# Loading the direct terms of the state space layer from the weights' queue, between the weights of the feed-forward network ahead of it

## The chip, the cores and the metric

The kernel runs on one core of a Trainium2 chip. The metric is device time in microseconds (us) of one launch. The engines of the core are TensorE (PE; its weight loads are listed apart as PEld), VectorE (DVE), ScalarE (ACT), GpSimd (POOL) and SyncE (SP); each executes its own row of instructions strictly in the order in which they stand. Transfers are issued from SP, ACT and POOL.

## What is computed

A stack of layers on a sequence of 256 tokens with 1024 features, in float32: stick-breaking attention, spatial gating, a state space layer (S5), attention again, each followed by a gated feed-forward network (FFN) with a short convolution; then a second block. What matters here is the second of these FFNs, called ffn1, and the S5 layer after it:

```
def conv_gated_ffn(xn, w_up, conv_w, conv_b, w_down):
    h = causal_depthwise_conv(xn @ w_up, conv_w, conv_b)
    a, g = jnp.split(h, 2, axis=-1)
    return (jax.nn.silu(g) * a) @ w_down
...
def s5_layer(...):
...
    _, _, xr, xi = lax.associative_scan(_complex_affine_combine, (a_re, a_im, bu_re, bu_im), axis=1)
    y = (jnp.einsum('ghp,blgp->blgh', c_re.astype(jnp.float32), xr)
         - jnp.einsum('ghp,blgp->blgh', c_im.astype(jnp.float32), xi))
```

The kernel computes the S5 scan in chunks of 8 tokens. Inside a chunk the answer of a group of 16 channels to its own inputs is one 128 x 128 matrix per group; these 64 matrices are the direct terms, `dT`. They depend on parameters alone.

## The kernel before

Activations lie transposed, features on the partitions. A matrix product is done in three passes for accuracy: the weights are split into a high and a low part (`wh`, `wl`), the activations too (`yh`, `yl`, or `hh`, `hl` for the hidden layer), and a block of 128 x 128 weights costs three matmuls of 256 columns, in the order `wh` with the high activations, `wh` with the low ones, `wl` with the high ones (`mm3`, L516 to L518).

**The stream of weights.** Eight blocks make a unit. For each unit there is one DMA of 512 KB on SP's queue (`_dma`, L352) into one of five staging tiles `st`, one ACT instruction that makes `wh` (L374), one DVE instruction that makes `wl` (L375), and then 24 matmuls. SP may load into `st` again when the `wl` of the unit that lay there is made. There are five `wh` and five `wl` tiles.

**ffn1** has 66 units, counted here from 0. `ffn_walk` goes through them as `ffn_order` says: 22 parts of the hidden layer, two units each (j = 0 to 21), and between them, from j = 4 on, the down products of parts that are done, two units after each pair of parts. So units 36 and 37 are part 13, units 38 and 39 a down product, 40 and 41 part 14. When PE has done part j, its activation follows as a chain over DVE and ACT (`act` in `ffn`): `pr` (DVE, L722), two `cv` on ACT (L725), four `cv` on DVE (L727), `sg` (ACT, L730), `hm` (DVE, L732), `hh` (ACT, L542), `hl` (DVE, L543).

**Work beside ffn1.** Tables and matrices that the S5 layer needs of its parameters are computed during the layers ahead of it, by a chain of generators `s.pre`, one of which is stepped on where `pre_step` is called (each step has a price, and a call pays for some). The last three are `s5_pre2` (products `O` and `A` on DVE, stored to `dB`), `s5_tables` (`s5mag`, `s5sin`, `s5cos`: DVE and ACT) and `s5_direct`: sixteen DMAs of 256 KB that read the matrix `dK` in device memory with a shift and write `dT`, issued by POOL (L1204). S5 uses `dT` in `y_mm` (L1302).

**What sets the order.** The code gives the instructions in program order with priorities; a scheduler of the tile layer then arranges each engine's row ahead of the run, by estimates of its own of when things become ready. `tc.keep_in_program_order` keeps an instruction from being moved on its engine. Once the program is built the rows are fixed.

Of the kernel before, what the change touches and what calls it, by code (L numbers as in the profile page):

```python
# [35 lines left out]
SBA, SBB, SBC = 4, 3, 1  # L36
EVG = 2
NSTEP = (2, 3)
DTC = 0.3
FEND = ((0, (18, 20)), (1, (18, 20)), (2, (18, 20)), (0, (20, 22)), (1, (20, 22)), (2, (20, 22)), (3, (18, 22)))  # L40
LATE = ((0, 1, 2, 3), (4, 5))
CY = (5, 2, 3, 2)
# [241 lines left out]
class Build:  # L284
    def __init__(s, ctx, tc, I, out, off, phases):
        s.tc, s.nc, s.I, s.out, s.ctx = tc, tc.nc, I, out, ctx
        nc = s.nc
        pool = lambda name, bufs, **k: ctx.enter_context(tc.tile_pool(name=name, bufs=bufs, **k))
        s.cp = pool("cp", 1)
        s.whp = pool("whp", WB)  # L290
        s.stp = pool("stp", NST)
        s.cq = pool("cq", 1)
        s.wlp = pool("wlp", WB)
        s.wk = pool("wk", 2)
        s.mm = pool("mm", MMB, space=PSUM)
        s.zp = pool("zp", 2, space=PSUM)
        s.pz = pool("pz", 1, space=PSUM)
        s.dp = pool("dp", 1, space=DRAM)
        s.bg = []
        s.pre = None  # L300
        s.credit = 0.0
        s.ahead = set()
        s.sin = None
        s.lowp = 0
        s.pin = 0
        s.want = 0
        s.phases = phases

        s.plan = []
        s.pos = -1  # L310
        s.cur = None
        s.ndma = 0
        s.nsp = 0
        s.tiles = {}

        w = I["consts"].shape[1]
        s.cp.tile([128, 48], F32, tag="gap", name="gap")
        s.cst = s.cp.tile([128, w], F32, tag="cst", name="cst")
        s.c = {k: s.cst[:, o:o + n] for k, (o, n) in off.items()}
        s.gs = s.cp.tile([128, 13 * 8], F32, tag="gs", name="gs")  # L320
        s.conv = s.cp.tile([128, 4, 4, 44], F32, tag="conv", name="conv")
        s.ssq = s.cp.tile([128, 2, T], F32, tag="ssq", name="ssq")
        s.rrow = s.cp.tile([128, T], F32, tag="rrow", name="rrow")
        s.idb = s.cp.tile([128, 128], BF, tag="idb", name="idb")
        s.msb = s.cp.tile([128, 128], BF, tag="msb", name="msb")
        s.msm = s.cp.tile([128, 128], BF, tag="msm", name="msm")
        s.x = s.cp.tile([128, KC, T], F32, tag="x", name="x")
        s.yh = s.cp.tile([128, KC, T], F32R, tag="yh", name="yh")
        s.yl = s.cp.tile([128, KC, T], F32R, tag="yl", name="yl")
        s.mcm = s.cp.tile([128, 2, 16], BF, tag="mcm", name="mcm")  # L330
        s.rcol = s.cq.tile([128, 2], F32, tag="rcol", name="rcol")
        s.g12 = s.cq.tile([128, 8], F32, tag="g12", name="g12")
        s.rcol2 = s.cq.tile([128, 2, 2], F32, tag="rcol2", name="rcol2")
        s.ss = s.cq.tile([128, 3, 2], F32, tag="ss", name="ss")
        s.cq.tile([128, 64], F32, tag="gap", name="gap")
# [336 lines left out]
    def ffn_walk(s, fp, act, resid, side):  # L672

        pre = s.norm_steps()
        P = None
        held = []
        H = {}
        acc = []
        nb = 0
        for x in ffn_order():  # L680
            if x[0] == "u":
                _, j, m, c = x
                if P is None:
                    P = s.ps().rearrange("p (m t) -> p m t", m=2)
                s.mm3(P[:, m], s.blk(), s.yh[:, c], s.yl[:, c], m == 0 and c == 0, c == KC - 1)
                nb += 1
                if nb in FSTEP:
                    next(pre)
                    if nb == FSTEP[1]:
                        pre = None  # L690
                if m == 1 and c == KC - 1:
                    held.append((j, P))
                    P = None
                    while held and pre is None:
                        k, Q = held.pop(0)
                        if k % 2 == 0:
                            H[k // 2] = [fp.tile([128, 2, T], F32R, tag=t, name=t, bufs=HB) for t in ("hh", "hl")]
                        act(k, Q, *[h[:, k % 2] for h in H[k // 2]])
                    if j < side[2]:
                        s.pre_step(side[0])  # L700
            else:
                _, n, c = x
                while not acc or n // 4 >= len(acc):
                    acc.append(s.zt())
                h, l = H[c // 2]
                b = acc[n // 4][:, n // 2 % 2].rearrange("p (m t) -> p m t", m=2)
                s.mm3(b[:, n % 2], s.blk(), h[:, c % 2], l[:, c % 2], n % 2 == 0 and c == 0, c == FT - 1)
                if n % 2 and c == FT - 1:
                    resid(n // 2, b)
                if n % 4 == 3 and c % 2 and c < side[2]:  # L710
                    s.pre_step(side[1])
# [483 lines left out]

    def s5_direct(s):

        while s.cpT is None:
            yield None
        for h in range(2):  # L1200
            s.dT[h] = s.cpT.tile([128, 32, 128], F32, tag="dT%d" % h, name="dT")
            src = s.dK[h * 32:h * 32 + 32, 0:16].rearrange("g h z k -> h g (z k)")
            for j in range(8):
                s.nc.gpsimd.dma_start(s.dT[h][j::8], src[:, :, (8 - j) * 16:(8 - j) * 16 + 128])  # L1204
                yield DTC

    def s5(s, nxt):
        nc = s.nc
# [642 lines left out]
    def run(s):  # L1851
# [15 lines left out]
        if "s5" in ph:  # L1867
            pool1, pool2, pool5 = ExitStack(), ExitStack(), ExitStack()
            tp = s.tc.tile_pool
            cp5 = pool5.enter_context(tp(name="cp5", bufs=1, side="right"))  # L1870
            s.s5cos = cp5.tile([128, 32, 32], F32, tag="s5cos", name="s5cos")
            s.s5sin = cp5.tile([128, 32, 32], F32, tag="s5sin", name="s5sin")
            s.s5mag = cp5.tile([128, 32], F32, tag="s5mag", name="s5mag")
            s.s5th = cp5.tile([128, 32], F32, tag="s5th", name="s5th")
            s.dT = [None, None]
            s.pre2_pool = None
            s.prep_pool = pool1.enter_context(tp(name="pre1", bufs=1))
            s.cpT = None
            s.pre = chain(s.s5_pre(), s.s5_pre2(), s.s5_tables(), s.s5_direct())
            s.pre_step(SIDE[7])  # L1880
        for i, p in enumerate(ph):
            if p == "s5" or "s5" in ph and ph[i + 1:i + 2] == ["s5"]:
                if s.cpT is None:
                    s.cpT = pool5.enter_context(tp(name="cpT", bufs=1, side="right"))
            if "s5" in ph and s.pre2_pool is None:
                s.pre2_pool = pool2.enter_context(tp(name="pre2", bufs=1))
            if p == "s5":
                s.pre_step(1e9)
                pool2.close()
                pool1.close()  # L1890
                if i == 0:
                    s.start_stream()
            nx = gi[ph[i + 1]] if i + 1 < len(ph) else None
            fin = 8 if i + 1 < len(ph) and ph[i + 1] == "mix2" else None
            if "mix2" in ph and i == max(0, ph.index("mix2") - 1):
                rope = ExitStack()
                s.pre = s.rope_tables(rope.enter_context(s.tc.tile_pool(name="rope", bufs=1, side="right")))
                s.credit = 0.0
            if p == "sb0" or p == "sb3":
                s.sb(int(p[2]), nx)  # L1900
            elif p == "sgu":
                s.sgu(nx)
            elif p == "s5":
                s.s5(nx)
                pool5.close()
            elif p == "mix2":
                s.pre_step(1e9)
                ld = s.tc.keep_in_program_order(s.nc.scalar.preload_act_table_set("exp_and_others"))
                with s.tc.issue_after(ld.ins):
                    s.mix2(nx, 8)  # L1910
                rope.close()
            elif p == "ffnx":
                if "ple" in ph:
                    s.ple_load(s.ctx.enter_context(s.tc.tile_pool(name="pl", bufs=1)))
                s.ffnx(nx)
            elif p == "ple":
                s.ple()
            else:
                s.ffn(int(p[3]), nx, fin)
# [28 lines left out]
```

## Time and profile before

| | us |
|---|---|
| median of 2 runs | 1616.78 (1616.11 to 1617.46) |
| profiled execution | 1621.75 |
| its span, first to last instruction | 1619.9 |
| busy PE, PEld, DVE, ACT, POOL | 1574.6, 1512.5, 1303.2, 948.5, 68.9 |

A row of the timeline gives start and length in us, engine, line, operation, what is written and read, and in square brackets how long the engine stood idle before it and what ended that. Rows of the windows give the busy time and the number of instructions of each engine in a stretch, the TensorE clock that was granted there (1.00 is 2.4 GHz, 0.50 is 1.2 GHz, between them a mixture), the share of the DMA engines and GB/s. Matmuls overlap: one row is 0.28 us long, the next starts 0.11 us later. Rows that follow each other on DVE or ACT overlap by about 0.1 us.

### The profile page before, as it was taken

The numbers are of one execution on the slowest core, as the hardware profiler recorded it, in microseconds if no ns is written. First come the engines' busy times: TensorE is split into PE (matmuls) and PEld (weight loads), VectorE is DVE, ScalarE is ACT, GpSimd is POOL, SyncE is SP. The second block draws the span as 40 slices with busy tenths as digits, with TensorE's granted clock in tenths as the row PEclk, the third lists the DMA queues.
The fourth block names the chain that finished last, engine by engine and source line by source line (L and its number), as shares of the span: only waits on it lengthen the run. The fifth ranks groups of instructions, "written<-read, shape, count | busy, mean of one in ns | idle before, by whom it ended". The sixth has DMA issues, their size and how long they took to land.

```text
span 1619.9 us, 33923 instructions
## 1 busy us (share of the span) xinstructions
PE 1574.6 (97%) x13644; PEld 1512.5 (93%) x13644; DVE 1303.2 (80%) x2380; ACT 948.5 (59%) x1481; POOL 68.9 (4%) x118
## 2 busy tenths in 40 slices
PE   7999999989999997999999999999999999999998
PEld 6999999979999996999999999999997899999998
DVE  8999998888999877788788558988886667766666
ACT  6777665645556651666566676655665546554444
POOL 0320100021120000000000000000000000000000
PEclk9999999999999997999999999999999999999999
DMA  7655767697996666756665434666554434666662
GB/s 262 202 172 178 232 210 224 198 298 222 263 252 229 219 194 201 259 173 207 196 195 187 153 129 144 203 201 195 159 174 137 149 112 133 200 192 193 195 195 79
DMA packets 95359, 312.55 MB, mean 193 GB/s; under 512 B 15057, under 2 KB 20689, under 8 KB 95201
## 3 DMA queue, kind: packets, MB, share of 16 engines
q1 hardware_dynamic: 82560, 282.21, 55.1%
q0 software_dynamic: 8480, 27.12, 5.9%
q8 instruction: 107, 1.75, 0.4%
q10 hardware_dynamic: 4160, 1.05, 0.3%
q14 instruction: 52, 0.42, 0.1%
HBM read 297.49 MB, written 12.85 MB: 192 GB/s over the span
## 4 chain that ended last, share of the span: by engine, by line
PE 72%; DVE 10%; issue 9%; DMA 5%; ACT 3%; POOL 0%; DVEq 0%; POOLq 0%; ACTq 0%; SPq 0%
PE mm L516 16%; PE mm L518 15%; PE mm L517 15%; PE z L517 5%; PE z L516 5%; PE z L518 5%; DVE wl L375 3%; DMA A<-s5bT_dram 1%; DMA st<-ffn_dram 1%; PE mm L530 1%; PE mm L531 1%; PE mm L529 1%; ACT wh L374 1%; PE z L818 1%; PE z L805 1%
## 5 line engine op out<-in xcount | busy, mean ns | idle before, releaser
L375 DVE TENSOR_TENSOR wl<-st,wh 128x1024 fp32r<-128x1024 f32 x508 | 618.2, 1220 | 156.1 <-ACT wh L374 155.3
L374 ACT CAST wh<-st 128x1024 fp32r<-128x1024 f32 x508 | 528.7, 1046 | 328.0 <-PE mm L517 207.3
L516 PE MATMUL mm<-yh,wh 128*128 128x256 f32 x2512 | 703.7, 280 | 2.9 <-ACT yh L568 1.9
L517 PE MATMUL mm<-yl,wh 128*128 128x256 f32 x2512 | 698.6, 278 | 1.4 <-DVE yl L569 0.9
L518 PE MATMUL mm<-yh,wl 128*128 128x256 f32 x2512 | 698.4, 278 | 1.0 <-DVE wl L375 1.0
L516 PEld LDWEIGHTS mm<-yh,wh 128*128 128x128 f32 x2512 | 473.5, 189 | 10.7 <-issue 6.4
L517 PEld LDWEIGHTS mm<-yl,wh 128*128 128x128 f32 x2512 | 474.1, 189 | 3.3 <-DVE yl L569 1.7
L518 PEld LDWEIGHTS mm<-yh,wl 128*128 128x128 f32 x2512 | 474.1, 189 | 1.7 <-DVE wl L375 1.6
L516 PE MATMUL z<-hh,wh 128*128 128x256 f32 x880 | 243.6, 277 | 0.3 <-ACT hh L542 0.3
L517 PE MATMUL z<-hl,wh 128*128 128x256 f32 x880 | 243.0, 276 | 0.4 <-DVE hl L543 0.4
L518 PE MATMUL z<-hh,wl 128*128 128x256 f32 x880 | 242.1, 276 | 0.0
L516 PEld LDWEIGHTS z<-hh,wh 128*128 128x128 f32 x880 | 165.1, 188 | 1.4 <-ACT hh L542 0.5
L517 PEld LDWEIGHTS z<-hl,wh 128*128 128x128 f32 x880 | 165.2, 188 | 0.6 <-DVE hl L543 0.6
L518 PEld LDWEIGHTS z<-hh,wl 128*128 128x128 f32 x880 | 164.8, 188 | 0.0
L727 DVE SCALAR_TENSOR_TENSOR cv<-pr,conv,cv 128x255 f32<-128x255 f32 (+1 forms) x352 | 147.1, 480 | 0.4
L542 ACT CAST hh<-hm 128x256 fp32r<-128x256 f32 x110 | 44.4, 405 | 121.5 <-DVE hm L732 96.6
L725 ACT ACTIVATE cv<-pr,conv 128x256 f32<-128x256 f32 x176 | 95.7, 593 | 16.6 <-DVE pr L722 16.6
L516 PE MATMUL mm<-oh,wh 128*128 128x256 f32 x320 | 89.8, 282 | 0.0
L517 PE MATMUL mm<-ol,wh 128*128 128x256 f32 x320 | 88.2, 277 | 0.0
L518 PE MATMUL mm<-oh,wl 128*128 128x256 f32 x320 | 88.2, 277 | 0.0
L722 DVE TENSOR_TENSOR pr<-mm,rrow 128x512 f32<-128x512 f32 x88 | 60.3, 689 | 13.1 <-PE mm L518 12.9
L543 DVE TENSOR_TENSOR hl<-hm,hh 128x256 fp32r<-128x256 f32 x110 | 46.0, 422 | 22.7 <-ACT hh L542 22.5
(453 smaller groups left out, 1848.2 us busy)
## 6 DMA issues: line engine op xcount, KB each, us to landing
st<-ffn_dram SPq DMA_DIRECT2D x264, 512.0 KB, 4.3
st<-ffnx_dram SPq DMA_DIRECT2D x66, 512.0 KB, 3.6
st<-sbqk_dram SPq DMA_DIRECT2D x32, 512.0 KB, 4.0
st<-sbv_dram SPq DMA_DIRECT2D x16, 512.0 KB, 4.3
st<-sbo_dram SPq DMA_DIRECT2D x16, 512.0 KB, 3.5
st<-s5glu_dram SPq DMA_DIRECT2D x16, 512.0 KB, 6.1
st<-m_g_dram SPq DMA_DIRECT2D x16, 512.0 KB, 3.6
st<-ple_dram SPq DMA_DIRECT2D x10, 512.0 KB, 3.6
```

The lines of the kernel that those rows point to most:

```text
L374: a = s.nc.scalar.copy(t[1][:, :n], t[0][:, :n])
L375: b = s.nc.vector.tensor_tensor(t[2][:, :n], t[0][:, :n], t[1][:, :n].bitcast(F32), OP.subtract)
L516: s.pinned(mm(P, w[0], xh, start=st, stop=False, skip_group_check=True))
L517: mm(P, w[0], xl, start=False, stop=False, skip_group_check=True)
L518: mm(P, w[1], xh, start=False, stop=sp, skip_group_check=True)
L529: s.pinned(mm(P[t][:, :width], a, w[0], start=c == 0, stop=False))
L530: mm(P[t][:, :width], a, w[1], start=False, stop=False)
L542: s.nc.scalar.copy(h, src)
L543: s.nc.vector.tensor_tensor(l, src, h.bitcast(F32), OP.subtract)
L722: nc.vector.tensor_tensor(pr, P, s.rrow.unsqueeze(1).to_broadcast([128, 2, T]), OP.mult)
L725: nc.scalar.activation(hc[:, m], pr[:, m], AF.Identity, bias=w(m, 3), scale=w(m, 2))
L727: nc.vector.scalar_tensor_tensor(hc[:, m, k:], pr[:, m, :T - k], w(m, 2 - k), hc[:, m, k:], OP.mult, OP.add)
```

## The change

`s5_direct` leaves the chain `s.pre`. It becomes a generator of its own, `s.direct`, made when ffn1 begins; after each part j of the hidden layer from j = 4 on (`DTJ`) `ffn_walk` steps it once. A step issues one of the sixteen DMAs, now from SP, and keeps it in program order there. What would be left is issued ahead of the S5 layer (nothing is: there are 18 such parts).

```
-DTC = 0.3
+DTJ = 4
...
                     if j < side[2]:
                         s.pre_step(side[0])
+                    if s.direct is not None and j >= DTJ:
+                        next(s.direct, None)
...
     def s5_direct(s):
 
-        while s.cpT is None:
-            yield None
         for h in range(2):
             s.dT[h] = s.cpT.tile([128, 32, 128], F32, tag="dT%d" % h, name="dT")
             src = s.dK[h * 32:h * 32 + 32, 0:16].rearrange("g h z k -> h g (z k)")
             for j in range(8):
-                s.nc.gpsimd.dma_start(s.dT[h][j::8], src[:, :, (8 - j) * 16:(8 - j) * 16 + 128])
-                yield DTC
+                s.tc.keep_in_program_order(
+                    s.nc.sync.dma_start(s.dT[h][j::8], src[:, :, (8 - j) * 16:(8 - j) * 16 + 128]))
+                yield
...
-            s.pre = chain(s.s5_pre(), s.s5_pre2(), s.s5_tables(), s.s5_direct())
+            s.pre = chain(s.s5_pre(), s.s5_pre2(), s.s5_tables())
...
                 if s.cpT is None:
                     s.cpT = pool5.enter_context(tp(name="cpT", bufs=1, side="right"))
+                    if p != "s5":
+                        s.direct = s.s5_direct()
...
             if p == "s5":
+                for _ in s.direct or s.s5_direct():
+                    pass
+                s.direct = None
                 s.pre_step(1e9)
```

The rows of the engines as built differ in more than the moved DMAs. Line numbers after the change are 1 to 7 higher, 3 higher in the activation (L725 becomes L728, L727 becomes L730).

SP, from the start of ffn1's loads on. Before, nothing but weights:

```order
L352 DMA st<-sgo_dram 128x1024 x8
L352 DMA st<-ffn_dram 128x1024 x66
L352 DMA st<-s5in_dram 128x1024 x6
L1176 DMA st<-dB 128x1024 x2
L352 DMA st<-s5in_dram 128x1024 x2
```

After:

```order
L353 DMA st<-sgo_dram 128x1024 x8
L353 DMA st<-ffn_dram 128x1024 x19
L1206 DMA dT<-dK 16x32x128
L353 DMA st<-ffn_dram 128x1024 x2
L1206 DMA dT<-dK 16x32x128
L353 DMA st<-ffn_dram 128x1024 x4
```

From there on a `dT` load stands after two and after four weight loads in turn, sixteen in all; the last has three weight loads of ffn1 behind it.

DVE, at the parts 12 and 13 of ffn1. Before, from the `hm` of part 12 to the `pr` of part 14; the `wl` are those of units 42, 43, 44 and 45:

```order
L732 TENSOR_TENSOR hm<-sg,cv 128x256
L722 TENSOR_TENSOR pr<-mm,rrow 128x512
L543 TENSOR_TENSOR hl<-hm,hh 128x256
L375 TENSOR_TENSOR wl<-st,wh 128x1024
L727 SCALAR_TENSOR_TENSOR cv<-pr,conv,cv 128x255 x2
L727 SCALAR_TENSOR_TENSOR cv<-pr,conv,cv 128x254 x2
L375 TENSOR_TENSOR wl<-st,wh 128x1024
L732 TENSOR_TENSOR hm<-sg,cv 128x256
L543 TENSOR_TENSOR hl<-hm,hh 128x256
L375 TENSOR_TENSOR wl<-st,wh 128x1024 x2
L722 TENSOR_TENSOR pr<-mm,rrow 128x512
```

After, the same stretch; the first two `wl` are those of units 37 and 38, the four together those of units 39 to 42:

```order
L376 TENSOR_TENSOR wl<-st,wh 128x1024
L735 TENSOR_TENSOR hm<-sg,cv 128x256
L376 TENSOR_TENSOR wl<-st,wh 128x1024
L544 TENSOR_TENSOR hl<-hm,hh 128x256
L725 TENSOR_TENSOR pr<-mm,rrow 128x512
L730 SCALAR_TENSOR_TENSOR cv<-pr,conv,cv 128x255
L730 SCALAR_TENSOR_TENSOR cv<-pr,conv,cv 128x254
L730 SCALAR_TENSOR_TENSOR cv<-pr,conv,cv 128x255
L730 SCALAR_TENSOR_TENSOR cv<-pr,conv,cv 128x254
L735 TENSOR_TENSOR hm<-sg,cv 128x256
L544 TENSOR_TENSOR hl<-hm,hh 128x256
L376 TENSOR_TENSOR wl<-st,wh 128x1024 x4
```

Where the `pr` of part 13 stood ahead of the `wl` of unit 42, it now stands ahead of those of units 39 to 42. The pattern repeats after each pair of parts to the end of ffn1.

ACT, the same place. Before, from the `wh` of unit 42 to those of units 44 to 46, around part 13:

```order
L374 CAST wh<-st 128x1024
L725 ACTIVATE cv<-pr,conv 128x256 x2
L374 CAST wh<-st 128x1024
L730 ACTIVATE sg<-cv 128x256
L542 CAST hh<-hm 128x256
L374 CAST wh<-st 128x1024 x3
```

After, from the `wh` of unit 38 to those of units 39 to 42:

```order
L375 CAST wh<-st 128x1024
L543 CAST hh<-hm 128x256
L728 ACTIVATE cv<-pr,conv 128x256 x2
L733 ACTIVATE sg<-cv 128x256
L543 CAST hh<-hm 128x256
L375 CAST wh<-st 128x1024 x4
```

The `wh` of unit 39 now stands behind the `hh` of part 13. The rows begin to differ at part 7, where the tables are computed: on DVE the `wl` of units 25 and 27 now stand behind runs of table operations.

## Rows read from the trace of the kernel before

**Rows 1.** Windows: stretch, length, busy us of each engine, clock, DMA share, GB/s.

```profile
487.00:496.00 9.00, 7.59 (x62) 7.00 (x61) 9.00 (x16) 5.17 (x7) 0.00 (x0) 1.00 0.86 312
...
520.00:580.00 60.00, 60.00 (x531) 60.00 (x531) 52.54 (x84) 38.33 (x58) 0.00 (x0) 1.00 0.66 209
```

**Rows 2.** Chain of work that ended last, between 500 and 560 us, by line.

```profile
by line: PE mm L518 24.4%; PE mm L516 23.9%; PE mm L517 23.7%; PE z L518 9.5%; PE z L516 9.4%; PE z L517 9.4%
```

**Rows 3.** Timeline of PE, 487 to 496 us: every wait there.

```profile
487.76 0.39 PE L518 MATMUL mm<-yh,wl 128*128 128x256 f32 x1 [0.19 <-DVE wl L375]
...
491.62 0.39 PE L518 MATMUL mm<-yh,wl 128*128 128x256 f32 x1 [0.82 <-DVE wl L375]
...
495.29 0.38 PE L517 MATMUL z<-hl,wh 128*128 128x256 f32 x1 [0.40 <-DVE hl L543]
```

**Rows 4.** Timeline of ACT, 476 to 492 us: the two longest waits for weights.

```profile
476.85 1.05 ACT L374 CAST wh<-st 128x1024 fp32r<-128x1024 f32 x1 [4.08 <-DMA st<-ffn_dram]
...
485.39 1.06 ACT L374 CAST wh<-st 128x1024 fp32r<-128x1024 f32 x1 [2.30 <-DMA st<-ffn_dram]
```

**Rows 5.** Timeline of POOL, 465 to 472 us: the last eight of sixteen loads.

```profile
465.55 1.28 POOL L1204 DMA_DIRECT2D dT<-dK  x2
467.39 3.71 POOL L1204 DMA_DIRECT2D dT<-dK  x6 [0.56 <-issue]
```

**Rows 6.** DMA issues of the whole run: KB each, median us to landing.

```profile
st<-ffn_dram SPq DMA_DIRECT2D x264, 512.0 KB, 4.3
...
dT<-dK POOLq DMA_DIRECT2D x16, 256.0 KB, 9.2
```

**Rows 7.** Groups of instructions, 500 to 560 us: count, busy us, mean ns, idle before.

```profile
L375 DVE TENSOR_TENSOR wl<-st,wh 128x1024 fp32r<-128x1024 f32 x25 | 30.3, 1222 | 4.3 <-ACT wh L374 4.3
L374 ACT CAST wh<-st 128x1024 fp32r<-128x1024 f32 x24 | 24.7, 1046 | 3.0 <-PE mm L517 3.0
...
L725 ACT ACTIVATE cv<-pr,conv 128x256 f32<-128x256 f32 x16 | 8.7, 592 | 2.9 <-DVE pr L722 2.9
...
L722 DVE TENSOR_TENSOR pr<-mm,rrow 128x512 f32<-128x512 f32 x8 | 5.5, 685 | 0.5 <-PE mm L518 0.5
L732 DVE TENSOR_TENSOR hm<-sg,cv 128x256 f32<-128x256 f32 x8 | 3.4, 421 | 0.0
...
L542 ACT CAST hh<-hm 128x256 fp32r<-128x256 f32 x8 | 3.3, 407 | 9.6 <-DVE hm L732 9.6
```

**Rows 8.** Timeline of DVE, 464 to 569 us: four rows that are used.

```profile
465.78 2.37 DVE L375 TENSOR_TENSOR wl<-st,wh 128x1024 fp32r<-128x1024 f32 x2
...
480.66 1.22 DVE L1156 TENSOR_TENSOR s5sin<-t,cst 128x1024 f32<-128x1024 f32 x1
...
485.31 0.68 DVE L931 SCALAR_TENSOR_TENSOR s5sin<-A,s5sin 128x512 f32<-128x512 f32 x1
...
563.09 1.66 DVE L727 SCALAR_TENSOR_TENSOR cv<-pr,conv,cv 128x255 f32<-128x255 f32 x4
```

**Rows 9.** Timeline of PE at 533 us: first matmuls of two blocks in a row.

```profile
533.31 0.28 PE L516 MATMUL mm<-yh,wh 128*128 128x256 f32 x1
...
533.65 0.28 PE L516 MATMUL mm<-yh,wh 128*128 128x256 f32 x1
```

**Rows 10.** Timeline of PE: two of its longer waits ahead of ffn1.

```profile
334.14 0.67 PE L594 MATMUL z<-dg,cst 128*128 128x256 f32 x2 [1.89 <-DVE dd L1063]
...
355.80 0.71 PE L882 MATMUL z<-wc,v 128*128 128x128 f32 x4 [3.16 <-DVE v L873]
```

**Rows 11.** Windows of 2 us behind those two waits; clock third from the end.

```profile
336.00:338.00 2.00, 2.00 (x23) 1.31 (x21) 2.00 (x6) 1.44 (x2) 0.74 (x1) 1.00 1.02 317
...
356.00:358.00 2.00, 2.00 (x15) 2.00 (x15) 2.00 (x4) 0.00 (x0) 0.00 (x0) 0.77 1.02 297
358.00:360.00 2.00, 2.00 (x12) 2.00 (x11) 0.99 (x3) 0.41 (x1) 0.00 (x0) 0.50 1.03 297
360.00:362.00 2.00, 2.00 (x17) 2.00 (x17) 1.23 (x3) 1.35 (x3) 0.00 (x0) 0.88 1.04 289
```

More of the change, by code (lines that the diff above doesn't have):

```diff
@@ L1887, in run @@
             if p == "s5":
+                for _ in s.direct or s.s5_direct():
+                    pass
+                s.direct = None
                 s.pre_step(1e9)
```

## Prediction

> **What bounds the kernel now.** I read ffn1 first by windows, because that is where every moved instruction stands. From 520 to 580 us PE is busy for the whole stretch and DVE for 52.5 of 60 us [rows 1], and the chain of work that ended last runs through PE alone there [rows 2]. So in ffn1 the time is the number of matmuls, as long as no unit of weights is late. It is late once: between 487 and 496 us PE waits three times, 0.19, 0.82 and 0.40 us, twice for `wl` [rows 3], and a step further back ACT waits up to 4.08 us for a weight load [rows 4]. This follows on the last eight `dT` loads, of which six are issued in 3.7 us [rows 5]. Hence the loads cost at most 1.4 us now. The other waits of the kernel lie outside what the change touches.
>
> How far the stream of weights runs ahead of PE is the quantity to look at. A block takes 0.34 us [rows 9], so a unit takes 2.72 us. PE reaches the `wl` of unit 30 at 487.76 [rows 3], the third matmul of that unit, so units start at 487.5 + 2.72 x (u - 30): unit 27 at 479.3.
>
> **The change, part by part.** *The sixteen DMAs.* Leaving POOL costs nothing there; POOL is idle most of the time, and nothing waits for these loads before the S5 layer. On SP they stand between weight loads. Each moves 256 KB, half of a weight load, and one comes per part, that is per 8.2 us, beside three weight loads. The DMA engines are busy for 0.66 of the time at 520 to 580 us [rows 1], and half a load for every three adds about a sixth of that, 0.11; this fits. A weight load behind a `dT` load can be late by the latter's landing: 9.2 us now, in a crowded stretch, against 4.3 us for a weight load of twice the size [rows 6]. Five staging tiles are 13.6 us of PE, so even 9.2 is covered, and I price it at zero. The 1.4 us of [rows 3] go, since the loads come one by one: **-1.4**.
>
> *The rows of DVE and ACT.* This part is not in the diff, but in the engines' rows, and it decides. Before, between units 26 and 65, the `wl` of a unit stands behind the `pr` of a part whose last unit is at least 3 and mostly 4 to 7 units older. After, that distance is 1 at twelve places: units 27, 31, 33, 37, 39, 43, 45, 49, 51, 55, 57 and 61. An engine can't overtake in its own row: `pr` waits till PE has finished the part, the `wl` waits behind `pr`, and PE, which has one unit left, waits for the `wl`. There are three kinds.
>
> Kind A (units 31, 37, 43, 49, 55, 61): between PE's end of the part and the `wl` stand `pr` 0.69, the first `cv` on ACT 0.59, four `cv` on DVE 1.66 and the `wl` itself 1.22 [rows 7, 8], 4.16 us, and 0.2 for the last matmul's end: 4.36. PE has one unit for that, 2.72, and two matmuls of the next block which need no `wl`, 0.22. It waits 1.4 us. Six times: **8.4**.
>
> Kind B (units 33, 39, 45, 51, 57): here `hm` and `hh` of the part stand ahead of the `wh` on ACT too. `pr` 0.69, `cv` 0.59, four `cv` 1.66, `hm` 0.42, `hh` 0.41, `wh` 1.05, `wl` 1.22 [rows 7, 8] are 6.04, with 0.2 as above 6.24; less 2.94, PE waits 3.3 us. (`sg` and `hl` run beside it.) Five times: **16.5**. Row overlaps of about 0.1 each could make it 2.9, handoffs 3.6.
>
> Kind C, the tables. Before, table operations stand one or two between each `wl`. After, the `wl` of unit 24 stands behind the `cv` of part 7, and those of units 25 to 27 behind most of the tables. The `wl` of units 23 and 24 run back to back from 465.78 to 468.15 [rows 8]; in the new row that of unit 24 ends some 1.5 later, at 469.7. From there I count to the end of unit 27's: three `wl` more at 1.15, nine operations on half a table at 0.3 to 0.6 (the upper end is a 0.68 row less the overlap), the whole table 1.22 [rows 8], ten on 32 columns at 0.1 to 0.2, two `pr`, two `hm`, two `hl`, seven `cv`: 15.5 us, so 485.2. PE wants it 0.2 into unit 27, at 479.5. It is 5.7 late, part of it at unit 25: **5.5**, between 3.5 and 6.5.
>
> Does something catch up in between? Behind kinds B four `wl` follow at 1.15 each while PE takes 2.72 for one, so the stock is rebuilt to three units, and then the next `pr` is ahead of the next `wl` again. The stock doesn't carry over, so the waits add up: 8.4 + 16.5 + 5.5 = **30.4**.
>
> *The clock.* After PE stood idle for 3.16 us ahead of 355.80 [rows 10], the granted clock was 0.77, 0.50 and 0.88 in the three windows behind it [rows 11]: 0.9, 2 and 0.5 us at the lower of the two levels, 3.4 us in all, which is 1.7 us of lost work. After an idle of 1.89 us ahead of 334.14 it stayed at 1.00 [rows 10, 11]. Kinds B (3.3) and C are nearer to the first row, kind A (1.4) to the second. I take 1.7 for five B and one C: **10.2**; the bounds are zero, if the clock holds each time, and this.
>
> Sum: -1.4 + 30.4 + 10.2 = +39.2. The profiled execution of 1621.75 (span 1619.9 and 1.85 around it) would become 1661; it lies 5.0 above the median of 1616.78, so the median becomes **1656**.
>
> **Rivals.** *Not slower.* The loads come evenly, the crowding goes, and PE doesn't feel the rows, because ACT and DVE are through before PE needs the unit. That decides at the chain: if it took under 2.94 us, less than half of the 6.24 that the rows give for B, no wait would be left. The time would be 1616.8 - 1.4 = 1615. For it: PE waited only 1.4 us in ffn1's second half, with a crowded DMA [rows 3]. Against it: it had 3 units in stock there. Beside this stands a rule of the Trainium skill, "DMA: Bandwidth & Descriptors", section "Issuing engine by pattern": queues of the sync and scalar engines are generally faster than GpSimd's. The trace agrees so far as 9.2 us from POOL stand against 4.3 from SP [rows 6], and by that rule alone this rival's time would come out. The section "Issuing engines are not separate DMA queues" says that the choice of the issuing engine only saves issue time, which would leave the median where it is.
>
> *The clock holds.* PE waits as worked out, but it isn't idle long enough for the lower level, since two matmuls split each B wait. 1616.8 + 29.0 = 1646; with B at 2.9 and C at 3.5 it is 1642.
>
> *SP blocks.* A `dT` load takes so long from SP that the weight load behind it arrives after its turn. The point is 13.6 us for a landing; 9.2 is what the rows show [rows 6]. If each second load came 4 us too late, 8 x 4 = 32 would come on top, partly in the same waits: 1656 + 16 = 1672 or more.
>
> *The change does nothing*: the loads land, the waits differ by less than a measurement sees: 1617.
>
> **How the numbers follow.** Forecast 0.56 (own range 1648 to 1664), clock holds 0.22, not slower 0.09, SP blocks 0.08, nothing 0.05. The range of 1634 to 1668 leaves out the two lasting cases without loss (0.14) and most of the blocked one. A change of under 2%, 32.3 us, is about what can't be told from none here. Above 1649.1 lie nearly all of the forecast and the blocked case and a little of the clock case: slower 0.60. Faster by 2% needs a gain of 32 us, for which there is no source: 0.02. The rest, 0.38, is within.
>
> **What would show it.** In the profile after: in ffn1 a wait of PE "for DVE wl" or "ACT wh" of 1 to 3.5 us twice per pair of parts, a pair lasting 21 to 23 us instead of 16.3, twelve places in all; ffn1 longer by 30 us or more, other layers unchanged; windows in ffn1 with a clock under 1.00, near six stretches of 3.4 us; DVE waiting for PE ahead of `pr`, which it hardly does now [rows 7]; ACT no longer waiting for weight loads; `dT` loads on SP landing within 9 us. The forecast is wrong if PE in ffn1 is as dense as now, or if its waits end on DMA.

## The result: 1655.98 us, slower by 2.5 per cent, and the profile after

The changed kernel takes 1655.98 us (two runs, 1654.61 and 1657.36) against 1616.78 before: a ratio of 1.0247, interval 1.0223 to 1.027. The profiled execution is the one of 1657.36, with a span of 1655.6.

The windows of the changed kernel, with the columns of [rows 1], at the same two places:

```profile
487.00:496.00 9.00, 8.87 (x75) 8.67 (x73) 4.23 (x9) 5.18 (x7) 0.00 (x0) 0.95 0.39 157
520.00:580.00 60.00, 46.20 (x350) 43.79 (x350) 36.65 (x56) 26.19 (x40) 0.00 (x0) 0.94 0.46 146
```

From 520 to 580 us PE issues 350 matmuls where it issued 531, DVE and ACT do a third less as well, and the DMA engines are busy for 0.46 of the time, not 0.66. All of them wait for each other in turn, and none is loaded more than before. From 487 to 495.9 PE doesn't wait any more; unit 31, which waited 0.82 us in [rows 3], now waits 0.75 just behind that, as a kind A. The chain of work that ended last, 500 to 560 us, ran through PE alone in [rows 2]:

```profile
by line: DVE cv L730 14.1%; PE mm L519 10.9%; DVE wl L376 10.3%; PE mm L517 9.7%; PE mm L518 9.5%; PE z L519 9.1%; PE z L518 6.7%; PE z L517 6.6%; DVE pr L725 5.8%; ACT wh L375 5.2%; ACT cv L728 5.1%; issue 4.4%; DVE hm L735 2.2%; ACTq L375
```

Now a part's activation and the weights' split stand in it, with PE between them. Where it breaks is told by PE's timeline:

```profile
480.65 0.38 PE L517 MATMUL z<-hh,wh 128*128 128x256 f32 x1 [2.94 <-ACT wh L375]
482.18 0.58 PE L517 MATMUL mm<-yh,wh 128*128 128x256 f32 x1 [1.03 <-ACT wh L375]
...
522.01 0.39 PE L519 MATMUL mm<-yh,wl 128*128 128x256 f32 x1 [1.15 <-DVE wl L376]
530.09 0.39 PE L517 MATMUL z<-hh,wh 128*128 128x256 f32 x1 [2.56 <-ACT wh L375]
531.35 0.39 PE L519 MATMUL z<-hh,wl 128*128 128x256 f32 x1 [0.76 <-DVE wl L376]
545.75 0.38 PE L519 MATMUL mm<-yh,wl 128*128 128x256 f32 x1 [1.15 <-DVE wl L376]
553.79 0.39 PE L517 MATMUL z<-hh,wh 128*128 128x256 f32 x1 [2.56 <-ACT wh L375]
```

The first two rows are the tables (kind C). Then the pattern repeats every 23.7 us, a pair of parts that took 16.3: one wait of 1.15 (kind A, with one of 0.13 ahead of it), then 2.56 and 0.76 (kind B). DVE's timeline shows why the second is longer; this is one kind B, from the end of part 13 to the `wl` of unit 39, for which PE waits at 531.35:

```profile
524.85 0.69 DVE L725 TENSOR_TENSOR pr<-mm,rrow 128x512 f32<-128x512 f32 x1 [1.08 <-PE mm L519]
526.21 1.92 DVE L730 SCALAR_TENSOR_TENSOR cv<-pr,conv,cv 128x255 f32<-128x255 f32 x4 [0.67 <-ACT cv L728]
528.23 0.43 DVE L735 TENSOR_TENSOR hm<-sg,cv 128x256 f32<-128x256 f32 x1
529.13 0.43 DVE L544 TENSOR_TENSOR hl<-hm,hh 128x256 fp32r<-128x256 f32 x1 [0.47 <-ACT hh L543]
530.07 2.36 DVE L376 TENSOR_TENSOR wl<-st,wh 128x1024 fp32r<-128x1024 f32 x2 [0.52 <-ACT wh L375]
```

`pr` had to wait for PE, everything else for `pr`, and PE for the `wl` at the end: from 524.85 to the end of the first `wl`, at about 531.3, are 6.4 us. (What the profile calls idle is less than what PE loses at such a place; the part on the prediction has the difference.) No load on the weights' queue is in this chain; ACT never waits for a weight load here. The sixteen loads landed sooner than before, and the weights no later (columns as in [rows 6]):

```profile
st<-ffn_dram SPq DMA_DIRECT2D x264, 512.0 KB, 4.2
...
dT<-dK SPq DMA_DIRECT2D x16, 256.0 KB, 5.2
```

The clock, in windows of 4 us that hold PE's busy time, the clock, the DMA share and GB/s:

```profile
480.00:484.00 4.00, 2.32 (x10) 0.64 0.14 32
484.00:488.00 4.00, 4.00 (x21) 0.50 1.00 301
...
532.00:536.00 4.00, 4.00 (x23) 0.57 0.82 247
...
544.00:548.00 4.00, 2.75 (x21) 1.00 0.28 86
...
556.00:560.00 4.00, 4.00 (x24) 0.57 0.90 235
...
580.00:584.00 4.00, 4.00 (x38) 1.00 0.95 282
```

Behind four of the five kinds B the clock falls (0.57 here), behind the fifth (577.49) and behind a kind A (545.75) it does not. Seven such windows are under 0.99 in ffn1 (0.64, 0.50, 0.63, 0.52, 0.57, 0.57, 0.58). The clock stood at the lower level (0.50) for 23.9 us in all, and PE was busy for 21.6 of them; at half the speed that is 10.8 us of lost work: 2.9 behind the tables, 2.9 at unit 33 (the first kind B), 1.6 to 1.7 at units 39, 45 and 57, none at unit 51.

### The profile page after: what moved, and what is told of

The parts are those of the page before. It is cut to its first block, busy times and chain, and to the rows that moved or that the text cites. A ratio compares the mean times of both kernels' runs of the same rounds, so it can differ in the third digit from the quotient of the medians.

```text
span 1655.6 us, 33915 instructions
## 1 busy us (share of the span) xinstructions
PE 1588.2 (96%) x13644; PEld 1520.8 (92%) x13644; DVE 1307.3 (79%) x2380; ACT 947.3 (57%) x1481; POOL 58.7 (4%) x102
## 4 chain that ended last, share of the span: by engine, by line
PE 79%; DVE 13%; ACT 3%; issue 3%; DMA 2%; POOL 0%; DVEq 0%; ACTq 0%; POOLq 0%
PE mm L517 17%; PE mm L519 17%; PE mm L518 16%; PE z L519 6%; PE z L517 5%; PE z L518 5%; DVE wl L376 4%; DVE cv L730 2%; ACT wh L375 1%; PE mm L530 1%; PE mm L532 1%; PE mm L531 1%; DVE pr L725 1%; DVE yl L570 1%; PE z L821 1%
## 5 line engine op out<-in xcount | busy, mean ns | idle before, releaser
L517 PE MATMUL z<-hh,wh 128*128 128x256 f32 x880 | 247.8, 282 | 15.0 <-ACT wh L375 14.2
L519 PE MATMUL z<-hh,wl 128*128 128x256 f32 x880 | 246.4, 281 | 3.9 <-DVE wl L376 3.9
L519 PEld LDWEIGHTS z<-hh,wl 128*128 128x128 f32 x880 | 168.3, 192 | 5.0 <-DVE wl L376 5.0
L518 PEld LDWEIGHTS z<-hl,wh 128*128 128x128 f32 x880 | 168.6, 192 | 0.0
L730 DVE SCALAR_TENSOR_TENSOR cv<-pr,conv,cv 128x255 f32<-128x255 f32 (+1 forms) x352 | 148.9, 479 | 8.5 <-ACT cv L728 7.4
L728 ACT ACTIVATE cv<-pr,conv 128x256 f32<-128x256 f32 x176 | 95.8, 593 | 79.0 <-DVE pr L725 79.0
L725 DVE TENSOR_TENSOR pr<-mm,rrow 128x512 f32<-128x512 f32 x88 | 60.3, 689 | 48.0 <-PE mm L519 47.7
L544 DVE TENSOR_TENSOR hl<-hm,hh 128x256 fp32r<-128x256 f32 x110 | 46.0, 422 | 23.7 <-ACT hh L543 23.6
```

The costliest lines, as they stand in the source:

```text
L517: s.pinned(mm(P, w[0], xh, start=st, stop=False, skip_group_check=True))
L518: mm(P, w[0], xl, start=False, stop=False, skip_group_check=True)
L519: mm(P, w[1], xh, start=False, stop=sp, skip_group_check=True)
L544: s.nc.vector.tensor_tensor(l, src, h.bitcast(F32), OP.subtract)
L725: nc.vector.tensor_tensor(pr, P, s.rrow.unsqueeze(1).to_broadcast([128, 2, T]), OP.mult)
L728: nc.scalar.activation(hc[:, m], pr[:, m], AF.Identity, bias=w(m, 3), scale=w(m, 2))
```

## Experiments

Theory 1: the rows cost the time. The new loads made the order of DVE's and ACT's rows come out differently, with a `wl` one unit behind the part whose `pr` precedes it. Theory 2: the loads themselves cost it, on the weights' queue or at the DMA engines; 39.2 us over sixteen loads are 2.45 each.

All kernels run the same 11,424 matmuls of 128x256 with split weights (`wh`, `wl`), so the time at which the n-th ended compares their stages. The stages are those of one profiled execution each, which can lie some us off the median beside them. In the table (us) ffn1 is the stretch from the 2700th, in ffn1's first parts, to the 4100th, shortly before its end; S5 is from there to the 4400th; rest is from there to the last.

| kernel | median | ffn1 | S5 | rest |
|---|---|---|---|---|
| before, first trace | 1616.78 | 162.2 | 74.2 | 955.3 |
| before, second trace (E5) | 1616.12 | 163.1 | 70.4 | 954.1 |
| changed kernel | 1655.98 | 204.6 | 71.8 | 953.3 |
| E1 changed, rows kept | 1624.28 | 169.1 | 73.9 | 952.7 |
| E2 nine loads | 1625.07 | 159.5 | 84.9 | 953.8 |
| E3 rows alone | 1686.53 | 224.8 | 71.0 | 964.8 |
| E4 ACT's row kept | 1627.61 | 174.3 | 71.6 | 953.7 |
| E6 sixteen spread | 1626.19 | 159.5 | 81.6 | 954.3 |
| E7 eight and eight | 1617.55 | 165.0 | 72.0 | 953.5 |
| E8 from part ten | 1655.49 | 176.3 | 97.2 | 957.4 |
| E9 eight paced | 1612.44 | 162.2 | 69.8 | 953.8 |
| E10 six early | 1614.11 | 161.0 | 71.8 | 955.2 |
| E11 one per part | 1629.63 | 176.3 | 70.8 | 953.6 |

The whole loss of the change, 41.5 us against the second trace of before, is in ffn1. The two traces of before show how far the same kernel varies: 0.9 us in ffn1, 3.8 in S5, 1.2 in the rest. Differences from before are taken to the second trace.

**E1 to E4: the loads and the rows, each without the other.** E1 keeps the sixteen loads where the change puts them and holds each part's chain behind the newest `wh` and `wl`:

```
+            s.last = a.ins, b.ins
...
+                        with ExitStack() as stack:
+                            for i in s.last if s.direct else ():
+                                stack.enter_context(s.tc.issue_after(i))
                             act(k, Q, *[h[:, k % 2] for h in H[k // 2]])
```

> The changed kernel with its sixteen loads where they are, on the weights' queue, but in ffn1 each part's activation chain is held behind the newest wh (on ACT) and wl (on DVE), so that a wl stands no nearer than 3 units behind the part whose pr precedes it. Theory 1 (the rows cost the time): PE's twelve waits go, the clock stays at 1.00, and the time is before's or that less 1.4: 1613 to 1619. Theory 2 (the loads themselves hold up the weights, on SP or at the DMA engines): the rows change nothing and the time stays at 1650 to 1660. If the stock of 3 units is too thin where before had 4 to 7, it lies between, 1620 to 1635.

Measured 1624.28, ratio to before 1.0051 (1.0036 to 1.0065). About four fifths of the loss are gone with the loads in place. The window of E1:

```profile
520.00:580.00 60.00, 59.87 (x528) 59.67 (x527) 49.93 (x79) 35.33 (x53) 0.00 (x0) 1.00 0.71 223
```

PE is as dense as before where the repeated waits were, with a `dT` load per part. What stays is the third case of the expectation, a stock that is too thin, but at a few places. Most of it is at the tables, with 3.5 us of the 5.9 that PE waits for weights in ffn1 and the only fall of the clock there (1.7 us); units 33 and 63 have most of the others. E1 keeps a distance of 3 units, but the `wl` of unit 27 still stands behind a run of table operations, and PE waits as at 480.65 above:

```profile
480.51 0.39 PE L518 MATMUL z<-hh,wh 128*128 128x256 f32 x1 [1.67 <-ACT wh L375]
482.86 0.58 PE L520 MATMUL z<-hh,wl 128*128 128x256 f32 x1 [1.85 <-DVE wl L376]
```

E2 steps the loads at every second part only; nine go out in ffn1, seven ahead of the S5 layer. The rows of DVE and ACT then come out as before.

```
-                    if s.direct is not None and j >= DTJ:
+                    if s.direct is not None and j >= DTJ and j % 2 == 0:
```

> One load after every second part: nine of the sixteen go out in ffn1 on the weights' queue, the last seven in one go ahead of the S5 layer. The rows of DVE and ACT stand in ffn1 as in the kernel before. Theory 1: no waits at the twelve places, 1613 to 1619. Theory 2: nine sixteenths of 39.2 us remain, 22 us, 1639.

Measured 1625.07, ratio 1.0058 (1.004 to 1.0076): again neither number. But ffn1 has no wait for weights at all and is 3.6 us shorter than before's; the S5 layer is 14.5 longer. PE's longest waits there:

```profile
603.38 3.63 PE L1271 MATMUL pz<-U,st 128*64 128x32 f32 x64 [2.54 <-DVE U L1262]
616.65 0.64 PE L1304 MATMUL z<-dT,U 128*32 128x128 f32 x4 [3.45 <-DVE U L1262]
631.60 1.19 PE L1308 MATMUL z<-st,S 128*32 128x128 f32 x16 [4.37 <-DMA st<-dC]
```

Loads left over stand ahead of that layer's own on SP, and the order of PE's rows in that layer has changed too. Which of the two costs the 14.5 us was not separated. By the traces they are 8.9 us of further waits (17.9 against 9.0) and 5.2 of lower clock (10.3 of lost work against 5.1).

E3 is the reverse: the kernel before, its loads on POOL, with the short distances made by hand.

```
+            if s.ahead_units < NS:
+                s.tc.keep_in_program_order(a)
+                s.tc.keep_in_program_order(b)
...
-        s.want = min(len(s.plan), s.pos + NS + 1)
+        s.want = min(len(s.plan), s.pos + s.ahead_units + 1)
...
                 _, j, m, c = x
+                s.ahead_units = 1 if late and 8 < j < 21 else NS
```

> The kernel before, loads on POOL as they were; only the rows are changed: from unit 26 to 57 wh and wl go out one unit ahead instead of three and behind the whole chain of the part. All ten places behind a part from unit 31 on are then of kind B. Theory 1: ten waits of 3.3 us are 33, the tables 4 to 6, the clock 2.4 us for each wait of that size that it answers to (four of five did in the changed kernel), up to 24: 1660 to 1680. Theory 2: no load stands on the weights' queue, so 1617.

Measured 1686.53. Without any load on the weights' queue ffn1 is 61.7 us longer than before's. The ten waits are there:

```profile
528.77 0.58 PE L520 MATMUL mm<-yh,wh 128*128 128x256 f32 x1 [2.56 <-ACT wh L375]
529.72 0.58 PE L520 MATMUL z<-hh,wh 128*128 128x256 f32 x1 [0.16 <-ACT wh L375]
540.49 0.38 PE L520 MATMUL z<-hh,wh 128*128 128x256 f32 x1 [2.58 <-ACT wh L375]
541.44 0.39 PE L520 MATMUL mm<-yh,wh 128*128 128x256 f32 x1 [0.45 <-ACT wh L375]
```

The time is 6.5 over the upper end: PE waits 9.0 at the tables where I had 4 to 6, and 10.7 us lie in later layers, whose rows the edit moved as well, which it was not meant to do.

E4 is E1 with ACT's row alone held: `act` runs within `issue_after(s.last[0])`, the `wh`, and DVE keeps its short distances.

> The changed kernel with the loads on the weights' queue and only ACT's row kept: the part's chain on ACT stands behind the newest wh; on DVE the wl still stands behind pr. Two wl then follow pr at kind A, 0.69 + 1.22 + 0.2 = 2.1 us, which is under 2.94: no wait. At kind B pr 0.69, hm 0.42, hh 0.41, wh 1.05, wl 1.22 and 0.2 are 4.0: 1.1 us, five times, with waits so short that the clock holds, and the tables 0 to 4. Theory 1 by this sum: 5 to 10 us over before, 1621 to 1628. Theory 2: 1650 to 1660.

Measured 1627.61, as theory 1 has it. Kind A is gone but for unit 61 (0.37 and 0.76), and of each kind B one wait is left, 0.76 where the sum gave 1.1. The rest is at the tables: PE waits 3.6 there, and the clock behind it costs 3.0, which the sum did not have. Two of the five kinds B:

```profile
521.50 0.39 PE L520 MATMUL z<-hh,wl 128*128 128x256 f32 x1 [0.76 <-DVE wl L376]
538.96 0.39 PE L520 MATMUL z<-hh,wl 128*128 128x256 f32 x1 [0.76 <-DVE wl L376]
```

So the distance in units does not decide by itself: what stands between `pr` and the `wl`, on both engines, does.

**E5** is the kernel before once more.

> The kernel before once more, for a second trace of it: its first profiled execution lay 5 us over its median. No theory speaks on it; 1612 to 1620.

Measured 1616.12. Its layers behind ffn1 are 4.9 us shorter than in the first trace of before, so the first profiled execution was long there, not in ffn1.

**E6 to E8: sixteen loads, other places.** E6 is a load after every second part from part 0, and five in ffn1's tail:

```
-                    if s.direct is not None and j >= DTJ:
+                    if s.direct is not None and j % 2 == 0:
...
+                if s.direct is not None and c > 15 and n % 2 and c % 2:
+                    next(s.direct, None)
```

> All sixteen loads on the weights' queue, eleven after every second part of ffn1 and five in its tail among the S5 layer's first weights. DVE's and ACT's rows stand in ffn1 as in the kernel before. Theory 1 (rows): no wait of PE for wl or wh in ffn1, which lasts some 5 us less than before as with nine loads; what is left is what the five late loads do to the S5 layer, five sevenths of the 13 us seen there with seven: 1613 to 1621. Theory 2 (loads): as many loads as in the changed kernel, 1650 to 1660.

Measured 1626.19, ratio 1.0063 (1.0043 to 1.0084), and again the two stages say more than the time: ffn1 159.5, with all sixteen loads on the weights' queue, the DMA engines busy for 0.81 of 520 to 580 us, and PE never late there:

```profile
520.00:580.00 60.00, 60.00 (x530) 59.93 (x530) 50.03 (x81) 36.24 (x56) 0.00 (x0) 1.00 0.81 237
```

This ends theory 2 for ffn1. The S5 layer, with the five late loads, is 11.2 us longer, where I expected five sevenths of 13; the time is 5 over theory 1's upper end.

E7 puts the first eight on POOL when the generator is first stepped, the last eight on SP at every second part:

```
-                s.tc.keep_in_program_order(
-                    s.nc.sync.dma_start(s.dT[h][j::8], src[:, :, (8 - j) * 16:(8 - j) * 16 + 128]))
-                yield
+                ld = (s.nc.gpsimd, s.nc.sync)[h].dma_start(s.dT[h][j::8], src[:, :, (8 - j) * 16:(8 - j) * 16 + 128])
+                if h:
+                    s.tc.keep_in_program_order(ld)
+                if h or j == 7:
+                    yield
```

> Eight loads from POOL in one go as before and eight on the weights' queue after every second part of ffn1; rows as in the kernel before, and no load close ahead of the S5 layer. Theory 1: the waits of PE at 487 to 496 us go, nothing else changes: 1609 to 1615, a little faster than before. Theory 2: half of 39 us, 1635. If the 9 us that nine loads cost came from ffn1 and not from the S5 layer, 1620 to 1625.

Measured 1617.55, ratio 1.0006 (0.9994 to 1.0018), no gain and 2.6 over theory 1's upper end. The waits near 490 are gone, but four loads now leave POOL together, where in the second trace of before two did at 433.80 and two at 447.21, and a new wait stands behind them. POOL's row and PE's:

```profile
433.84 2.51 POOL L1205 DMA_DIRECT2D dT<-dK  x4
...
451.30 0.58 PE L519 MATMUL mm<-yh,wl 128*128 128x256 f32 x1 [3.63 <-DVE wl L376]
```

E8 is the changed kernel with `DTJ = 10`.

> The changed kernel with the loads after parts 10 to 21 only, four of them in one go ahead of the S5 layer. Short distances are left at two places of kind B (units 51 and 57) and two of kind A (55 and 61); up to unit 49 a wl that stands one unit behind has only a pr ahead of it, which fits. Theory 1: PE waits 2 x 3.3 + 2 x 1.2 = 9, the clock 0 to 5, restarts 1, and the four late loads 0 to 7 in the S5 layer; less 3 to 5 for the waits at 487 to 496: 1620 to 1635, with no wait of PE ahead of unit 51. Theory 2: sixteen loads as in the changed kernel, 1650 to 1660.

Measured 1655.49: wrong by 20 us and more, though not by theory 2's mechanism. In ffn1 the loss is 13.2 us; the waits are B, A, B, A at units 51, 55, 57 and 61 as forecast, none ahead of them, and one more of B's size (2.97 and 0.46) at unit 65, which lies behind the 4100th matmul and so in the table's S5. That column is 26.8 us longer, 3.4 of them unit 65; in the S5 layer itself late loads again stand and PE's rows again moved; I had priced that at 7.

**E9 to E11: the clean dose.** To leave the S5 layer out of it, E9 puts the first eight loads back on POOL in the chain `s.pre`, spaced as before, and only the last eight on SP, after every second part; PE's rows are then those of before throughout.

```
-    def s5_direct(s):
+    def s5_direct(s, h):
+        while s.cpT is None:
+            yield None
...
+            ld = (s.nc.gpsimd, s.nc.sync)[h].dma_start(s.dT[h][j::8], src[:, :, (8 - j) * 16:(8 - j) * 16 + 128])
+            if h:
+                s.tc.keep_in_program_order(ld)
+            yield DTC
...
+            s.pre = chain(s.s5_pre(), s.s5_pre2(), s.s5_tables(), s.s5_direct(0))
...
+                        s.direct = s.s5_direct(1)
```

> The first eight loads stand on POOL where they stand in the kernel before, the last eight (there in one go at 465 to 470 us) go out on the weights' queue after every second part of ffn1. Rows as in the kernel before. Theory 1: the waits of PE at 487 to 496 us go, 1.4 to 3 us, and nothing comes in: 1612 to 1615, faster by 0.1 to 0.2 per cent. Theory 2: half of 39 us, 1635.

Measured 1612.44 against 1616.96 for the kernel before on the same chip, ratio 0.9971 (0.996 to 0.9982): faster than both kernels, by 4.5 us where theory 1 had 1.4 to 3. E9 at the two stretches of [rows 1], PE without a gap, and its two waits for weights elsewhere in ffn1, at units 16 and 21:

```profile
487.00:496.00 9.00, 9.00 (x82) 9.00 (x81) 9.00 (x17) 4.51 (x7) 0.00 (x0) 1.00 0.63 182
520.00:580.00 60.00, 60.00 (x532) 60.00 (x531) 51.96 (x83) 38.01 (x58) 0.00 (x0) 1.00 0.72 220
...
450.79 0.39 PE L520 MATMUL mm<-yh,wl 128*128 128x256 f32 x1 [1.19 <-DVE wl L377]
465.33 0.39 PE L520 MATMUL z<-hh,wl 128*128 128x256 f32 x1 [0.64 <-DVE wl L377]
```

So the waits at 487 to 496 are gone as forecast, but "nothing comes in" does not hold: before's second trace waits 0.44 at unit 16 and not at unit 21. By the traces ffn1 is only 0.9 us shorter than before's, and E9's traced execution (1615.56) was the slowest of its nine; where the rest of the 4.5 us lies is not shown.

E10 sends six from POOL early and ten from SP after every second part from part 2 on.

> Six loads from POOL early, ahead of ffn1 (four of them in one go), ten on the weights' queue after every second part of ffn1 from part 2 on. Rows as in the kernel before. Theory 1: no wait in the second half of ffn1, 1611 to 1615, unless four loads in one go make a wl late as they did at 451 us in the run with eight and eight, then 1615 to 1618. Theory 2: ten sixteenths of 39 us, 1640.

Measured 1614.11, ratio 0.9979 (0.9968 to 0.999), as theory 1 has it; against E9 no difference can be told. Four loads leave POOL together here too, and no `wl` is late within 45 us of them:

```profile
415.02 2.52 POOL L1205 DMA_DIRECT2D dT<-dK  x4
...
463.31 0.39 PE L519 MATMUL z<-hh,wl 128*128 128x256 f32 x1 [0.95 <-DVE wl L376]
```

E11 is E9 with the eight loads one after each part, from part 8 on (`DTJ = 8`, without `j % 2`).

> As the kernel with eight paced loads, but these eight go out one after each part, from part 8 on, as the changed kernel spaces them; PE's order and the S5 layer stay as before. The short distances return at five units; by the rows ahead of them two are of kind B (45 and 51) and one of kind A (49), the other two have only a pr ahead. Theory 1: PE waits 2 x 3.3 + 1.2 = 7.8, restarts 0.5, the clock 0 to 4.8, less 1.4 to 3: 1619 to 1627, with the waits at units 45, 49 and 51 and none elsewhere. Theory 2 in either form (each load, or each load at this spacing, costs 2.45): 1635.

Measured 1629.63, ratio 1.008 (1.0065 to 1.0095): 2.6 over theory 1's range, 5.4 under theory 2's number. PE's timeline tells which:

```profile
533.44 0.39 PE L518 MATMUL z<-hh,wh 128*128 128x256 f32 x1 [2.57 <-ACT wh L376]
534.70 0.39 PE L520 MATMUL z<-hh,wl 128*128 128x256 f32 x1 [0.76 <-DVE wl L377]
549.05 0.39 PE L520 MATMUL mm<-yh,wl 128*128 128x256 f32 x1 [1.15 <-DVE wl L377]
557.14 0.39 PE L518 MATMUL z<-hh,wh 128*128 128x256 f32 x1 [2.57 <-ACT wh L376]
558.40 0.39 PE L520 MATMUL z<-hh,wl 128*128 128x256 f32 x1 [0.76 <-DVE wl L377]
```

B, A and B, at units 45, 49 and 51, with the sizes of the changed kernel to 0.01 us. What I had missed is 1.5 us more at unit 39, which I had counted as fitting, and 0.55 at unit 37. E9 and E11 send the same eight loads by the same queue; their spacing moves the rows, and the rows move the time by 17 us.

## Why the prediction was right

The forecast of 1656 holds, and by its mechanism: the late units are the twelve that it named, for the reason that it gave, and E1, E3 and E6 show rows and loads apart. That it hits the median to a tenth is luck. By the traces the stretch grew by 41.5 us, 10.8 of them the clock (forecast 10.2) and 30.7 the stops of PE (forecast 29.0); the difference of the medians happens to be 39.2.

- **The sixteen DMAs at zero:** right. They landed in 5.2 us, no wait of PE or ACT ends on DMA in ffn1 from 420 us on, and E6 carries all sixteen there at no cost. **The -1.4** was too small: with all crowding gone and the rows kept (E2, E6) ffn1 is 3.6 shorter than before's second trace, which has 2.2 us of such waits, one of them at 448 us, and 2.7 shorter than its first.
- **Kind A, 8.4:** printed 0.75, four times 1.15, and 1.16, that is 6.5, with 0.13 more ahead of each. What PE loses is larger. When part 12 is done, PE has unit 36 in stock; the first row here is where it starts it, and the `wl` matmul of unit 37, for which it then waits, starts at 522.01 (above). The last row is the start of unit 38, the unit in stock ahead of the kind B at unit 39:

```profile
517.34 0.28 PE L517 MATMUL mm<-yh,wh 128*128 128x256 f32 x1
...
517.54 0.69 DVE L725 TENSOR_TENSOR pr<-mm,rrow 128x512 f32<-128x512 f32 x1 [7.24 <-PE mm L519]
518.91 1.92 DVE L730 SCALAR_TENSOR_TENSOR cv<-pr,conv,cv 128x255 f32<-128x255 f32 x4 [0.67 <-ACT cv L728]
520.74 1.22 DVE L376 TENSOR_TENSOR wl<-st,wh 128x1024 fp32r<-128x1024 f32 x1
...
524.65 0.28 PE L517 MATMUL z<-hh,wh 128*128 128x256 f32 x1
```

  From 517.34 to 522.01 are 4.67 us where the sum had 4.36; the four `cv` took 1.92, not 1.66. A unit and two matmuls take 2.94, so 1.73 us are lost, not 1.4.
- **Kind B, 16.5:** printed 2.79 + 0.46 once and 2.56 + 0.76 four times, 16.5 to the tenth, and this is luck. From the last row above (524.65) to the `wl` matmul at 531.35 are 6.70 us where the sum had 6.24, so 3.76 are lost, not 3.3.
- **Kind C, 5.5:** printed 2.94 + 1.03 = 4.0, in its range of 3.5 to 6.5. Unit 27 starts at 479.02 in the trace of before, 0.3 earlier than I worked out.
- **The stock does not carry over:** right. The waits repeat at full size to the end, and E3 and E11 get the same size from other numbers of them.
- **The clock, 10.2:** 10.8 lost, but not as six times 1.7: two places lost 2.9, three 1.6 to 1.7, one none. E11's two lost 1.7 each, as the row did from which the term was taken.
- **Missing from the sum:** what a stop costs beyond the idle time that the timeline prints. At each kind A and B (unit 33 apart, which met the lower clock too) the unit in stock and the two matmuls take 3.38 us with the printed waits left out, not 2.94, since the row ahead of a wait counts as busy for 0.28 where the next one would start after 0.11, and the row behind a wait lasts 0.39. All printed waits are 27.9 us (27.0 in eighteen, 0.9 in seven of 0.10 to 0.14); with 10.8 of clock and less the 2.2 of before they make 36.5 of the 41.5. Eleven times 0.44, 4.8, is nearly all of the other 5.0.

*Not slower* fell to the 6.4 us of the chain. These loads did land sooner from SP (5.2 us against 9.2), and nothing waits for them. The Trainium skill, "DMA: Bandwidth & Descriptors", section "Issuing engine by pattern", says that the sync engine's queue is generally faster than GpSimd's. How much of this is the queue is not shown, since the loads also came one by one: two from POOL at 448 us in the trace of before landed in 4.9 and 6.6 us; four in one go took 5.3 to 8.2 from SP (E8) and 6.4 to 13.1 from POOL (E7), beside different traffic. *The clock holds* fell to the windows. *SP blocks* fell to E1 and E6. Of the signs named, the twelve places, the loads' landing, ACT no longer waiting for weights and DVE waiting for PE ahead of `pr` are there; a pair lasts 23.7 us, not 21 to 23, with the clock and those 0.44 us in it.

Open stays why the S5 layer loses 11 to 23 us where loads were left for its start, loads or rows (E2, E6, E8). PE's waits in that column add up to 9.0 us in E5, 17.9 in E2, 18.2 in E6 and 24.9 in E8, and the lower clock costs 5.1, 10.3, 5.8 and 15.3, which is nearly all of it; of the waits 1.6, 5.2, 1.4 and 4.9 end on a DMA, so most of what was added ends on DVE or ACT. E1's S5 of 73.9 lies between the two traces of before and says nothing. That the scheduler's picture of the weights' queue moves the rows is argued from E9 against E11, where only the spacing of the loads differs; no run shows how it comes to its order.

## What to carry to other kernels

Where a scheduler arranges the rows ahead of the run, a DMA that is moved to the queue of the weights can move the rows of engines that the edit never names. After such an edit, compare the rows of each compute engine, not only the DMAs: look for work that refills a stock and now stands behind work that waits for its consumer. Price it by the length of that chain less what the consumer still has in stock, and take it from the starts of the rows, not from the printed idle time alone. Keep to a spacing of the loads that leaves the rows alone; here eight loads, one at every second part, gained 0.3 per cent, and one at every part lost 0.8.

## What the runs showed of the hardware that was not expected

Equal waits do not always get an equal answer of the clock: behind 2.56 + 0.76 us of idle PE in the changed kernel the window showed 0.57 at 532 and at 556 us, and 1.00 at 580, behind 577.49, where the waits were the same. In E4 a single 0.76 never moved it (1.00 from 520 to 528 us).

Sixteen loads of 256 KB on the weights' queue, one by one but for the last five, made no weight late in ffn1 (E6). Of four issued by POOL within 2.5 us the runs say two things: 17 us behind them a `wl` was 3.63 us late in E7, and none was within 45 us in E10. So the burst alone does not decide; what else does is not shown.
